# A second buffer for the output weights' pieces, one attention buffer less, and pooled operands issued behind copies

## The chip, the cores and the metric

The kernel runs on one core of a Trainium2 chip. The metric is the device time of one execution in microseconds (us). The engines carry the profile's names: PE is TensorE (matrix products), PEld its weight loads, DVE is VectorE, ACT is ScalarE, POOL is GpSimd, and SP is the engine that issues most of the DMAs. Engines run side by side and wait for each other by semaphores. Within one engine, instructions run in the order in which they were laid out when the program was built, so an instruction that waits holds up all that stand behind it on its engine.

## The reference, cut to what matters

One decoder layer over 1024 tokens of width 2048, all in float32. Every name below is an input or an intermediate of the reference.

```python
h = jnp.einsum('bsd,dc->bsc', x, w_in) + b_in
q, k, v, g_attn, u_pool, g_pool = jnp.split(h, SPLIT_POINTS, axis=-1)
a = banded_sink_attention(q, k, v, sinks, bias_hqk, valid) * jax.nn.silu(g_attn)
b = multiscale_pool(u_pool, w_pool, pool_scale) * jax.nn.silu(g_pool)
mix = jnp.einsum('bsc,cd->bsd', jnp.concatenate([a, b], axis=-1), w_out)
ple = jax.nn.sigmoid(jnp.einsum('bsd,de->bse', x, w_gate_ple)) * jnp.einsum('bsp,pd->bsd', p_i, w_ple)
return layer_norm(DEEPNORM_ALPHA * x + mix + ple, ln_gain, ln_bias)
```

The attention has 16 heads of width 64 and 2 key/value heads. Each block of 128 queries sees its own and the previous block of 128 keys, through a mask with a relative-position bias (`bias_hqk`, laid out for the kernel as `rel`), and each head has a sink that enters the softmax's maximum and sum. The pooling mixer takes trailing means over 2, 4, 8 or 16 tokens, subtracts the token and multiplies by a small matrix per group.

## The kernel before

**Products.** Every large product is done in blocks by a scheme with seven block products in place of eight, and every float32 operand is split into a high and a low part (`wh`, `wl`; an operand unit `t3` gives `t3h`, `t3l`), so that one block product is three matmuls for each of four slices of the inner dimension: 12 matmuls of 128x512 into a PSUM bank `qa` or `qb` (`mm3`, L180 to L185; `product`, L463). A `Job` is a pair of output blocks over half of the inner dimension; `run_group` (L441) runs the seven products of one job, or the fourteen of two jobs in turn. The operand units of the left side are `b11`, `b21`, `t1`, `t2`, `t3`, `b22`, `t4`, used in this order (`BESIDE`, L48, where `t1` and `t2` may change places).

After its last product into a bank, the bank is copied or added into the tile `part` (`gather`, L418 to L425: a copy on ScalarE for the first, an addition on VectorE for the others). The bank can be used again when that has been done.

**Weights.** A job's two weight blocks are loaded into tiles `raw` by SP (`feed_raw`, L194; five buffers), summed and subtracted in place on VectorE (`three_sums`, L206), and split into `wh` (a cast on ScalarE, L816) and `wl` (a subtraction on VectorE, L126) four products ahead of their use (`make_unit`, L215; `take`, L248).

**The clock.** `self.clock` counts products. `after(n, fn)` (L159) runs `fn` when n more products have been written out; `later(n, fn)` (L167) does the same, but ties each instruction of `fn` behind the instruction last recorded on its own engine (`mark`, L134: the last product's matmul on PE, and the last copies on ACT and additions on DVE). The code is thus interleaved by hand into the product loop. Each instruction then gets its place on its engine from a planner that works when the program is built: it goes by the order of the code, but it may put an instruction ahead of others whose operands or buffers are not free yet. `issue_after` is what `later` uses to forbid that.

**Stages.** The products for q, k and v come first. In the attention stage, from about 180 to 700 us, the products go on while other work is hung between them:

- 16 calls of `heads` (L575), one every 9 products, each for four heads and 256 queries. One call: `begin` loads the queries and the two masks (`bias`, from `in_rel`); `split` splits the queries; `score` (L604) multiplies queries by keys into bank `sc`, and VectorE adds the mask and takes the maximum (L616); `shift`, `softmax` and `share` make the shares; `trans` (L644) transposes them into bank `tr`, splits them and masks out their older half on GpSimd (L656); `value` (L659) multiplies by the values into bank `pv`. The steps from `score` on come twice, for n = 0 and n = 1, 4 products apart. All of its buffers are taken from the pool `slots0`, 15 buffers of 128x512 float32 in rotation.
- `centre_weights` (L937) takes the mean over the output columns off `w_out`. It loads `w_out` in 32 pieces of 256 KB into a tile `cw` and sums each on VectorE (`add_up`, L948, line L950), then loads the 32 pieces again, subtracts the mean and stores them as `wc` (`centre`, L956). One piece is fetched every 2 products (every 2 or 3 in the second pass), and used 2 products behind its fetch; the pool `cw` has one buffer.

The third stage makes the gates, the pooling and the embeddings, and ends at about 1107 us. The fourth stage multiplies by the first half of `w_out`; its left operands, the pooled ones, are made by `set_by_twos` (L395) during the last 21 products of the third stage and the first 14 of the fourth. `make_pooled` is the list of its seven steps, for the units in the order above, at the products (10, 13, 16, 19, 22, 28, 31) counted from 21 products ahead of the fourth stage (L1336 to L1338). A step splits a unit (two casts of 128x1024 on ScalarE, two subtractions on VectorE) and issues the loads of the unit two places on. The fifth and sixth stages multiply by the centred half, `wc`, and the norm follows.

`self.ones` (L1268) is a tile of ones that `norm_sums` (L1023) multiplies by, of which it reads one column.

Of the kernel before, what the change touches and what calls it, by code (L numbers as in the profile page):

```python
# [24 lines left out]
F32 = mybir.dt.float32  # L25
# [6 lines left out]
P = 128  # L32
T = 512
H = 4 * P
# [31 lines left out]
class Layer:  # L66
# [203 lines left out]
    def two(self):  # L270
        return self.tile(self.twos, [P, 2, self.F], "two")
# [303 lines left out]
    def heads(self, h, j, half):  # L575
# [9 lines left out]
        def begin():  # L585
            f = slice(h * T + 256 * half, h * T + 256 * half + 256)
            q = self.slot()[:, :T]
            rq.append(q)
            for i in range(2):
                self.load(two(q)[:, i], self.qd[j + i][:, f])  # L590
            for i in range(2):
                bias.append(self.slot()[:, :T].rearrange("p (e k) -> p e k", e=2))
                self.load(bias[i], self.rel[j + i])
# [10 lines left out]
        def score(n, i):  # L604
            s = sc[n, i] = self.slot()[:, :T].rearrange("p (e k) -> p e k", e=2)
            ps = self.bank("sc", 2, (P, 2, 256))
            z = P if none(n) else 0

            keys = slice((4 * h + block(n) - 1) * P + z, (4 * h + block(n) + 1) * P)
            for e in range(2):  # L610
                q = qs[e][:, 256 * i + n * P : 256 * i + n * P + P]
                for k, kk in enumerate(self.kk):
                    nc.tensor.matmul(ps[:, e, z:], q, kk[:, keys], start=k == 0, stop=k == 1)  # L613
            for e in range(2):
                c = 4 * n + 2 * i + e
                nc.vector.tensor_tensor_reduce(  # L616
                    out=s[:, e, z:], in0=ps[:, e, z:], in1=bias[i][:, e, z:], op0=ALU.add, op1=ALU.max, scale=1.0,
                    scalar=self.c(C_SINK + 8 * (j + i) + 2 * block(n) + e), accum_out=mx[:, c : c + 1])
# [19 lines left out]
        def share(n, i):  # L638
            cur = sc[n, i][:, :, P:]
            for e in range(2):  # L640
                c = 4 * n + 2 * i + e
                nc.scalar.activation(cur[:, e], cur[:, e], AF.Copy, scale=rec[:, c : c + 1])
# [16 lines left out]
        def value(n):  # L659
            ps = self.bank("pv", 1)  # L660
            ms = [(self.vv[h][:, block(n)], t) for t in pt[n]]
            if not none(n):
                ms += [(self.vd[h][:, block(n) - 1 + h], t) for t in old[n]]
            for i, (w, t) in enumerate(ms):
                nc.tensor.matmul(ps, w, t, start=i == 0, stop=i == len(ms) - 1)  # L665
            if not pre:
                pre.append(two(self.slot()[:, :T]))
            low = self.slot()[0:64, :T]
            nc.scalar.copy(out=low, in_=ps[64:128])
            hi, low = (t.rearrange("p (i e q) -> p i e q", i=2, e=2) for t in (ps[0:64], low))  # L670
            for e in range(2):
                self.tt(pre[0][64 * e : 64 * e + 64, :, n * P : n * P + P], hi[:, :, e], low[:, :, e], ALU.add)
            if n:
                f = slice(h * T + 256 * half, h * T + 256 * half + 256)
                for i in range(2):
                    self.load(self.pre[j + i][:, f], pre[0][:, i])

        begin()
        self.later(3, split)
        for n in range(2):  # L680
            for i in range(2):
                self.after(6 + 4 * n, lambda n=n, i=i: score(n, i))
            self.after(9 + 4 * n, lambda n=n: shift(n))
            self.after(15 + 4 * n, lambda n=n: trans(n))
            for i in range(2):
                self.after(10 + 4 * n, lambda n=n, i=i: softmax(n, i))
                self.later(12 + 4 * n, lambda n=n, i=i: share(n, i))
            self.after(21 + 4 * n, lambda n=n: value(n))


    def gate_ahead(self, j):
# [245 lines left out]
    def centre_weights(self, at, by):  # L937

        nc = self.nc
        cells = [(b, h) for b in range(NB) for h in range(2)]  # L940
        sums = self.fix.tile([P, 8, NB], F32, name="wsum")
        mean = self.fix.tile([P, 8], F32, name="wmean")
        now = []

        def fetch(b, h):
            now.append(self.load(self.tile(self.cw, [P, H], "cw"), self.wout[b, 0][:, h * H : h * H + H]))

        def add_up(b, h):  # L948
            k = now.pop().rearrange("p (k m) -> p k m", k=4)
            nc.vector.reduce_sum(sums[:, 4 * h : 4 * h + 4, b : b + 1], k, axis=mybir.AxisListType.X)  # L950

        def take_mean():
            nc.vector.reduce_sum(mean.rearrange("p (k b) -> p k b", b=1), sums, axis=mybir.AxisListType.X)
            nc.vector.tensor_scalar(out=mean, in0=mean, scalar1=1.0 / D, scalar2=None, op0=ALU.mult)

        def centre(b, h):  # L956
            w = now.pop()
            k = w.rearrange("p (k m) -> p k m", k=4)
            m = mean[:, 4 * h : 4 * h + 4].rearrange("p (k m) -> p k m", m=1).broadcast_to([P, 4, P])
            self.tt(k, k, m, ALU.subtract)  # L960
            self.load(self.wc[b, 0][:, h * H : h * H + H], w)

        for step in (add_up, centre):
            for c in cells:
                self.after(at, lambda c=c: fetch(*c))
                self.later(at + 2, lambda c=c, step=step: step(*c))
                at += by if step is centre and c[0] % 3 else 2
            if step is add_up:
                self.later(at + 1, take_mean)
                at += 2  # L970

    def split_total(self, total, w, cut):
# [50 lines left out]
    def norm_sums(self, sums, a, first, last):  # L1023

        for b in range(a.shape[-1] // P):
            self.nc.tensor.matmul(sums[:, b : b + 1], a[:, b * P : (b + 1) * P], self.ones[:, 0:1], start=first and b == 0, stop=last,
                                  skip_group_check=True)

    def norm_scale(self, L, wait=0):
# [55 lines left out]
    def run(self):  # L1085
        nc, tc, fix = self.nc, self.tc, self.fix
# [101 lines left out]
        parts, work, over = ExitStack(), ExitStack(), ExitStack()  # L1188
# [76 lines left out]
        self.turn.clear()  # L1265
        self.ident = fix.tile([P, P], F32, name="ident")
        make_identity(nc, self.ident)
        self.ones = fix.tile([P, P], F32, name="ones")  # L1268
        nc.gpsimd.memset(self.ones, 1.0)
        self.mhalf = fix.tile([P, 8], F32, name="mhalf")  # L1270
        nc.gpsimd.memset(self.mhalf, -0.5)
# [10 lines left out]
        work = ExitStack()  # L1282
        self.new_part = lambda b: self.tile(pp, [P, 2, T], "part")
        self.slot_n = T
        self.slots = self.work_pool("slots0", 15, work)
        self.kv = self.work_pool("kv", 1, over)

        def build_kv(b, build, group, halves=(0, 1)):
# [24 lines left out]
        for i in range(n3):  # L1313
            if i == 1:
                over.close()
                work.close()
                work, over = ExitStack(), ExitStack()
                self.slot_n = T + 16
                self.slots = self.work_pool("slots", 16, work)
                self.extras = self.work_pool("e2", 6, over)  # L1320
            if self.groups[g + i + 1][0][0].b[0] == 4 and i < n3 - 2:
                self.after(5, self.embed_in)
                self.after(7, lambda: self.embed_w(2))
            if i == n3 - 2:

                over.close()
                work.close()
                work = ExitStack()
                self.slot_n = T
                six[:] = 5 * [pp] + 3 * [self.work_pool("p8", 3, work)]  # L1330
                self.slots = self.work_pool("slots1", 8, work)
                self.twos = self.work_pool("twos1", 4, work)
                self.new_part = part_of_six
                for n, b in enumerate(s3[-4].b + s3[-3].b):
                    self.after((1, 1, 5, 6)[n], lambda b=b: self.gate_ahead(b - GA0))
                pooled()  # L1336
                for n, step in enumerate(make_pooled):
                    self.after((10, 13, 16, 19, 22, 28, 31)[n], step)  # L1338
                for n, b in enumerate(b for j in s3[-2:] for b in j.b):
                    self.after(16 + 2 * n, lambda b=b: self.gate_ahead(b - GA0))  # L1340
            first = self.groups[g + i][0][0]
            if first.w is wgate and first.b[0] in (4, 6, 8, 10):
                self.pool_sums(*divmod(first.b[0] // 2 - 2, 2), kept_pool)
            self.run_group(g + i, () if i else steps)
# [25 lines left out]
        for i in range(n4):  # L1370
            if i == 1:
                work.close()
                work = ExitStack()
                at = next(i for i, p in enumerate(six) if p is not pp)
# [155 lines left out]
```

## Time and profile before

| What | Value |
|---|---|
| Median of 3 runs | 1445.88 us |
| The three runs | 1445.77, 1445.88, 1448.65 us |
| The profiled execution, its own time | 1448.33 us |
| Its span, first to last instruction | 1446.6 us |
| PE, DVE, ACT, POOL busy | 1429.2, 1115.5, 792.1, 232.8 us |
| DMA moved | 311.86 MB, 216 GB/s over the span |
| Granted TensorE clock, mean | 0.996 |

A row of a group or of the timeline names start and duration in us, the engine, the line of the kernel, the operation, and output `<-` inputs by the program's tile names; a bracket at the end gives the idle time of that engine just before the instruction, and whose signal ended it. A row of the waits names who waited for whom, then the total in us, the count and the longest. A row of the windows names a stretch of the span, then for PE, PEld, DVE, ACT and POOL the busy us and the count of instructions, and then the granted clock, the DMA engines' busy share and GB/s. Durations of matmuls overlap: the distance from one matmul's start to the next is what a matmul costs.

### The profile page before, as it was taken

How to read it: one execution, taken by the hardware profiler on the slowest of the kernel's cores; microseconds unless marked ns; L12 is line 12 of the kernel's file. 1: busy time of each engine (PE TensorE's matmuls, PEld its weight loads, DVE VectorE, ACT ScalarE, POOL GpSimd, SP SyncE). 2: the span in 40 equal slices, each digit the busy share in tenths (PEclk: the TensorE clock that was granted, in tenths of full speed). 3: DMA queues.
4: the chain of work that ended last, by engine and by line, in shares of the span. 5: the costliest groups of instructions: out<-in, count | busy, mean ns of one | idle time of the engine just before them, and what ended most of it. 6: DMA issues, size and time to landing. Idle time of an engine off the chain costs nothing.

```text
span 1446.6 us, 20400 instructions
## 1 busy us (share of the span) xinstructions
PE 1429.2 (99%) x6820; PEld 1210.5 (84%) x6820; DVE 1115.5 (77%) x2045; ACT 792.1 (55%) x1565; POOL 232.8 (16%) x339
## 2 busy tenths in 40 slices
PE   9999999999999999999999999999999999999996
PEld 7888887888888888888888888888888888899996
DVE  6859567787788877878768876867678665987787
ACT  6546375665667656665664444443356433654476
POOL 0000202211122211212111211211001211111223
PEclk9999999999999999999999999999999999999998
DMA  9463877455456655566887869998699768494566
GB/s 358 180 240 120 233 204 225 154 180 177 159 192 200 206 176 184 196 212 211 219 248 210 227 206 287 343 274 266 193 303 308 218 179 232 131 280 111 118 238 228
DMA packets 119226, 311.86 MB, mean 216 GB/s; under 512 B 13585, under 2 KB 27281, under 8 KB 119121
## 3 DMA queue, kind: packets, MB, share of 16 engines
q1 hardware_dynamic: 94480, 230.08, 46.5%
q0 software_dynamic: 21312, 73.15, 21.4%
q10 hardware_dynamic: 3328, 7.34, 1.5%
q8 instruction: 53, 0.87, 0.2%
q14 instruction: 53, 0.43, 0.1%
HBM read 211.95 MB, written 98.57 MB: 215 GB/s over the span
## 4 chain that ended last, share of the span: by engine, by line
PE 90%; DMA 4%; issue 2%; DVE 2%; ACT 1%; POOL 0%; POOLq 0%; SPq 0%; DVEq 0%; ACTq 0%
PE qa L183 15%; PE qa L185 15%; PE qa L184 15%; PE qb L185 11%; PE qb L183 11%; PE qb L184 11%; DMA part<-r 2%; PE sc L613 2%; PE pv L665 2%; DMA cw<-in_wout 2%; PE sc L185 1%; PE sc L183 1%; PE sc L184 1%; PE tr L649 1%; DVE wl L126 0%
## 5 line engine op out<-in xcount | busy, mean ns | idle before, releaser
L816 ACT CAST wh<-raw 128x512 fp32r<-128x512 f32 x428 | 264.3, 619 | 402.9 <-PE qa L184 156.6
L126 DVE TENSOR_TENSOR wl<-raw,wh 128x512 fp32r<-128x512 f32 x428 | 295.2, 693 | 105.2 <-ACT wh L816 100.3
L423 ACT COPY part<-qa 128x512 f32<-128x512 f32 (+1 forms) x180 | 104.0, 578 | 83.9 <-PE qa L185 81.5
L126 DVE TENSOR_TENSOR part<-part,qb 128x512 f32<-128x512 f32 (+1 forms) x120 | 81.1, 676 | 45.2 <-PE qb L185 40.6
L183 PE MATMUL qa<-b11h,wh 128*128 128x512 f32 (+2 forms) x292 | 108.9, 373 | 0.4 <-ACT part L423 0.4
L183 PE MATMUL qb<-b21h,wh 128*128 128x512 f32 (+2 forms) x292 | 108.9, 373 | 0.0
L185 PE MATMUL qa<-b11h,wl 128*128 128x512 f32 (+2 forms) x292 | 108.7, 372 | 0.0
L185 PE MATMUL qb<-b21h,wl 128*128 128x512 f32 (+2 forms) x292 | 108.7, 372 | 0.0
L184 PE MATMUL qa<-b11l,wh 128*128 128x512 f32 (+2 forms) x292 | 108.6, 372 | 0.0
L184 PE MATMUL qb<-b21l,wh 128*128 128x512 f32 (+2 forms) x292 | 108.5, 372 | 0.0
L183 PE MATMUL qa<-t3h,wh 128*128 128x512 f32 (+1 forms) x260 | 100.5, 387 | 2.2 <-ACT part L423 2.2
L184 PE MATMUL qa<-t3l,wh 128*128 128x512 f32 (+1 forms) x260 | 100.3, 386 | 0.0
L185 PE MATMUL qa<-t3h,wl 128*128 128x512 f32 (+1 forms) x260 | 100.3, 386 | 0.0
L183 PE MATMUL qa<-t2h,wh 128*128 128x512 f32 (+1 forms) x260 | 100.1, 385 | 0.1
L183 PE MATMUL qb<-t1h,wh 128*128 128x512 f32 (+1 forms) x260 | 99.9, 384 | 0.0
L185 PE MATMUL qa<-t2h,wl 128*128 128x512 f32 (+1 forms) x260 | 99.8, 384 | 0.0
L183 PE MATMUL qb<-b22h,wh 128*128 128x512 f32 (+1 forms) x260 | 99.7, 384 | 0.0
L185 PE MATMUL qb<-t1h,wl 128*128 128x512 f32 (+1 forms) x260 | 99.7, 384 | 0.0
L185 PE MATMUL qb<-b22h,wl 128*128 128x512 f32 (+1 forms) x260 | 99.7, 383 | 0.0
L185 PE MATMUL qa<-t4h,wl 128*128 128x512 f32 (+1 forms) x260 | 99.7, 383 | 0.0
L183 PE MATMUL qa<-t4h,wh 128*128 128x512 f32 (+1 forms) x260 | 99.6, 383 | 0.0
L184 PE MATMUL qb<-t1l,wh 128*128 128x512 f32 (+1 forms) x260 | 99.6, 383 | 0.0
(336 smaller groups left out, 3494.3 us busy)
## 6 DMA issues: line engine op xcount, KB each, us to landing
raw<-in_win SPq DMA_DIRECT2D x65, 512.0 KB, 4.2
h<-part SPq DMA_DIRECT2D x34, 512.0 KB, 3.0
part<-h POOLq DMA_DIRECT2D x34, 512.0 KB, 6.6
cw<-in_wout SPq DMA_DIRECT2D x64, 256.0 KB, 3.0
raw<-in_wgate SPq DMA_DIRECT2D x32, 512.0 KB, 4.9
raw<-wc SPq DMA_DIRECT2D x32, 512.0 KB, 4.4
s<-in_x SPq DMA_DIRECT2D x44, 256.0 KB, 5.7
s<-in_rel SPq DMA_DIRECT2D x32, 256.0 KB, 4.3
```

Of the source, the lines that this page charges most:

```text
L126: return (eng or self.nc.vector).tensor_tensor(out=out, in0=a, in1=b, op=op)
L183: mm(ps, wh, xh, start=start, stop=False, skip_group_check=True)
L184: mm(ps, wh, xl, start=False, stop=False, skip_group_check=True)
L185: return mm(ps, wl, xh, start=False, stop=stop, skip_group_check=True)
L423: self.mark("ACT", self.nc.scalar.copy(out=dst, in_=ps))
L613: nc.tensor.matmul(ps[:, e, z:], q, kk[:, keys], start=k == 0, stop=k == 1)
L649: nc.tensor.transpose(ps[:, o : o + P], sc[n, i][:, e, P:], self.ident)
L665: nc.tensor.matmul(ps, w, t, start=i == 0, stop=i == len(ms) - 1)
L816: ins = self.nc.scalar.copy(out=out, in_=a)
```

## The change

Five edits.

1. `centre_weights` gets a second buffer, the pool `cw2`; `fetch` takes the two in turn, and `now` becomes a queue, first in, first out. Each piece is used three products behind its fetch in place of two (`add_up` and `centre`), and `take_mean` comes one product later.
2. The pool `slots0` has 14 buffers in place of 15.
3. In `heads`, the two mask loads leave `begin` and come two products later; `value` comes one product earlier, for n = 0 and n = 1.
4. The steps that split the pooled units `b22` and `t4` are hung in with `later` in place of `after`, at products 27 and 30 in place of 28 and 31.
5. `self.ones` is 128x1 in place of 128x128, and `norm_sums` takes it whole.

```diff
@@ heads
             for i in range(2):
                 self.load(two(q)[:, i], self.qd[j + i][:, f])
+
+        def masks():
             for i in range(2):
                 bias.append(self.slot()[:, :T].rearrange("p (e k) -> p e k", e=2))
                 self.load(bias[i], self.rel[j + i])
...
         begin()
+        self.after(2, masks)
         self.later(3, split)
...
-            self.after(21 + 4 * n, lambda n=n: value(n))
+            self.after(20 + 4 * n, lambda n=n: value(n))
@@ centre_weights
-        now = []
+        now, cws = [], [self.cw, self.cw2]
 
         def fetch(b, h):
-            now.append(self.load(self.tile(self.cw, [P, H], "cw"), self.wout[b, 0][:, h * H : h * H + H]))
+            cws.append(cws.pop(0))
+            now.insert(0, self.load(self.tile(cws[0], [P, H], "cw"), self.wout[b, 0][:, h * H : h * H + H]))
...
                 self.after(at, lambda c=c: fetch(*c))
-                self.later(at + 2, lambda c=c, step=step: step(*c))
+                self.later(at + 3, lambda c=c, step=step: step(*c))
                 at += by if step is centre and c[0] % 3 else 2
             if step is add_up:
-                self.later(at + 1, take_mean)
+                self.later(at + 2, take_mean)
                 at += 2
@@ norm_sums
-            self.nc.tensor.matmul(sums[:, b : b + 1], a[:, b * P : (b + 1) * P], self.ones[:, 0:1], start=first and b == 0, stop=last,
+            self.nc.tensor.matmul(sums[:, b : b + 1], a[:, b * P : (b + 1) * P], self.ones, start=first and b == 0, stop=last,
                                   skip_group_check=True)
@@ run
-        self.ones = fix.tile([P, P], F32, name="ones")
+        self.ones = fix.tile([P, 1], F32, name="ones")
...
-        self.slots = self.work_pool("slots0", 15, work)
+        self.slots = self.work_pool("slots0", 14, work)
+        self.cw2 = self.work_pool("cw2", 1, work)
...
                 for n, step in enumerate(make_pooled):
-                    self.after((10, 13, 16, 19, 22, 28, 31)[n], step)
+                    (self.later if n > 4 else self.after)((10, 13, 16, 19, 22, 27, 30)[n], step)
```

## The prediction

> **What bounds the kernel now.** I read the page's first part, then TensorE's waits, then three windows around the largest of them.
>
> ```profile
> span 1446.6 us, 20400 instructions
> PE 1429.2 (99%) x6820; PEld 1210.5 (84%) x6820; DVE 1115.5 (77%) x2045; ACT 792.1 (55%) x1565; POOL 232.8 (16%) x339
> PE qa L183 <- ACT part L423: 2.7, 2, 2.2
> ...
> PE sc L613 <- DVE st L616: 0.3, 1, 0.3
> 230.00:235.00 5.00, 4.40 (x20) 3.31 (x18) 4.93 (x16) 1.57 (x7) 0.29 (x1) 1.00 0.94 232
> 235.00:240.00 5.00, 3.35 (x8) 2.68 (x9) 2.04 (x7) 4.68 (x10) 1.15 (x2) 0.68 0.95 235
> 240.00:245.00 5.00, 5.00 (x28) 4.24 (x28) 4.10 (x12) 1.20 (x2) 1.61 (x2) 0.98 0.86 326
> ```
>
> TensorE is busy for 99% of the span, so only its pauses can be won. The waits left out of the list are those of the kernel's first and last steps, which the diff leaves alone, and some of at most 0.2 us. The L183 waits are two (total, count and longest in us): one near 236 us, where the granted clock (the column after POOL's) also falls to 0.68, and a small one. This is the first:
>
> ```profile
> 229.50 0.69 DVE L950 TENSOR_REDUCE wsum<-cw 128x4 f32<-128x512 f32 x1 [2.20 <-DMA cw<-in_wout]
> 233.43 0.21 ACT L625 ACTIVATE st<-st 128x4 f32<-128x4 f32 x1 [3.76 <-DVE st L126]
> 234.01 0.39 PE L185 MATMUL qb<-t1h,wl 128*128 128x512 f32 x1
> 236.02 0.57 ACT L423 COPY part<-qa 128x512 f32<-128x512 f32 x1
> 236.65 0.67 PE L183 MATMUL qa<-t3h,wh 128*128 128x512 f32 x1 [2.25 <-ACT part L423]
> 237.11 0.63 PE L184 MATMUL qa<-t3l,wh 128*128 128x512 f32 x1
> 240.40 0.39 PE L183 MATMUL qa<-t3h,wh 128*128 128x512 f32 x1
> 1107.26 0.39 PE L184 MATMUL qa<-t4l,wh 128*128 128x512 f32 x1
> 1107.48 0.39 PE L185 MATMUL qa<-t4h,wl 128*128 128x512 f32 x1
> ```
>
> Read backwards. TensorE needs bank qa, which ScalarE copies out at 236.02. ScalarE had stood 3.76 us for VectorE's softmax shift. VectorE had stood 2.20 us before the reduction of a weight piece whose load had not landed. An undisturbed step from matmul to matmul is 0.22 to 0.23 us (last two rows); I use 0.227, so a product of 12 matmuls is 2.72 us. The pause costs 236.65 - 234.01 - 0.23 = **2.41 us**. The nine steps to 240.40 take 3.75 us in place of 9 x 0.227 = 2.04: **1.71 us** at the lower clock.
>
> The Trainium skill, page "TensorE: Matmul & The Clock Gate", section "Part 1: The HAM clock gate", puts the halving behind an idle window of about 3.4 us. By that section, 2.25 us of idleness would not lower the clock, and the 1.71 us would have another cause and stay. Here the first long step stands right behind the pause, so the row goes against the page's figure.
>
> **The change part by part.** *Second buffer cw2, use three products behind the load.* These rows are the landing times of the tile cw, waits of VectorE (190 to 240 us) and SP (190 to 720 us), and the chain of waits:
>
> ```profile
> DMA to landing us min/median/max: 2.0/2.9/9.3
> DVE wsum L950 <- DMA cw<-in_wout: 7.2, 4, 3.6
> SPq L140 <- DMA cw<-in_wout: 71.4, 31, 9.0
> SPq L140 <- PE pv L665: 21.2, 8, 6.3
> 202.57 9.30 DMA cw<-in_wout
> 270.50 0.95 PE sc L613 x8
> 286.51 0.95 PE sc L613 x8
> 299.80 0.96 PE sc L613 x8
> ```
>
> Scores of one kind come every 9 products: 299.80 - 270.50 = 29.3 us, or 3.26 us per product with attention in it. With one buffer, a load may start only behind the reduction placed at the same tick, and its own reduction stands two products later: at most 6.5 us, less whatever VectorE is late. The four loads of the crowded stretch took up to 9.3 us, so VectorE stood 7.2 us. With two buffers the load waits for a reduction placed one product earlier, and is used 3 x 3.26 = 9.8 us behind its place. Even 9.3 us fits. The last wait alone, 2.20 us, is nearly the pause; with all 7.2 us gone the copy at 236.02 comes before TensorE asks. I count -2.41 and -1.71. What is late next is VectorE's own list, 4.93 of 5 us busy from 230 to 235: a few tenths could stay. SP, which stood 71.4 us on cw, issues what is queued behind it sooner. Number and size of the 64 loads, 32 reductions and 32 stores do not change. Each use moves by one product, past what SP issues in that product; the centred pieces are then stored a product later, and the stage that reads them begins hundreds of us behind. No cost.
>
> *14 attention buffers, masks later, value one product earlier.* A head takes 9 products before the next begins. Two mask buffers held two products less and eight share buffers held one less are 12 buffer-products per 9 products, or 1.3 buffers of demand, against the one taken away. The mask's lead:
>
> ```profile
> 264.86 1.79 SPq L140 DMA_DIRECT2D s<-in_rel  x2
> DMA to landing us min/median/max: 2.8/4.3/9.3
> 299.36 0.44 PE tr L649 x4
> 319.47 0.92 PE pv L665 x4
> ```
>
> The masks issued at 264.86 serve the scores at 286.51, 21.6 us later. Two products (6.5 us) off leaves 15.1, against at most 9.3 to landing (the second row is that of the masks). On SP the two loads of each of the 16 heads move past what two products issue there (a cw piece, weight blocks, stores of `h`); nothing is added. `value` takes its two `pre` stores along, a product earlier. The values of the transposes at 299.36 run at 319.47, 20 us behind; one product less is 17. Between stand a cast, a subtraction and two selections on GpSimd, which is busy 16% of the span. Cost nothing; if that cover failed, TensorE would pause at L665. The order on each engine is laid out when the program is built, and this shifts it: the trace of before can't show the new one. Bounds: from -0.4 us (the 0.3 us score wait goes, with its step) to +4.1 us for one new pause of the kind at 236. I take 0, the nearer row, since in all the rest of the attention stage TensorE waits once, for 0.3 us.
>
> *Pooled operands b22 and t4 behind copies.* The small wait:
>
> ```profile
> 1106.70 1.05 ACT L816 CAST b22h<-two 128x1024 fp32r<-128x1024 f32 x1 [2.62 <-DMA two<-cc]
> 1107.65 0.58 ACT L423 COPY part<-qa 128x512 f32<-128x512 f32 x1
> 1108.28 0.50 PE L183 MATMUL qa<-b11h,wh 128*128 128x512 f32 x1 [0.41 <-ACT part L423]
> 1108.62 0.39 PE L184 MATMUL qa<-b11l,wh 128*128 128x512 f32 x1
> 1107.78 1.23 DVE L126 TENSOR_TENSOR b22l<-two,b22h 128x1024 fp32r<-128x1024 f32 x1 [2.44 <-ACT b22h L816]
> 1135.63 0.39 PE L183 MATMUL qb<-b22h,wh 128*128 128x512 f32 x1
> ```
>
> The second of b22's two casts waits 2.62 us for its operand, and the bank copy queues behind it. The loss is 1108.28 - 1107.48 - 0.23 = 0.57 us, and 0.11 in the step behind it. `later` ties the casts behind the copies recorded by then, and so adds a wait: behind it on ScalarE queue casts of weight units, which are made four units ahead. The operands' loads are issued by earlier steps and do not move. The 27th product falls six into the stage begun at 1108.28, at 1124.6; two casts and the last subtraction (2 x 1.05 + 1.23 = 3.3 us) fit before 1135.63. t4 at the 30th (1132.8) is needed two products after b22, at 1141.1. So **-0.6 us**, a tenth left for a bank's handing over. If that cover failed, TensorE would pause there for some tenths instead: 0 net.
>
> *ones, one column wide.*
>
> ```profile
> L1269 POOL MEMSET ones<- x1: 205/205/205, 0.9 to 0.9; 128x128 f32 x1
> ```
>
> By the code the matmuls read one column already. 0.2 us of fill on GpSimd lie beside the first weight loads. Nothing.
>
> **Sum.** -2.41 - 1.71 - 0.6 = -4.7 us on the profiled execution's 1448.33 (1446.6 of span and 1.7 around it): **1443.6 us**. The runs shown lie at 1445.77, 1445.88 and 1448.65. The profiled one belongs with the highest; the 2.45 us to the median are the size of the slow clock (1.71) and a part of the pause. I read that as a pause that lowers the clock in some executions only. Against the median 1445.88 the forecast is -0.16%. A measurement of this kernel tells about 0.2%, or 2.9 us, from no change: faster begins below 1443.0, slower above 1448.8.
>
> **The rivals.**
>
> *The pause is not what the runs differ by.* Then the median holds all 4.7 us, and the time is 1445.88 - 4.7 = 1441.2. For it: no trace of a short run is shown. Against: the sizes match.
>
> *SP is held by a mask instead* (the slower side). With 14 buffers a mask's load waits on SP for a buffer that `value` frees, and weight blocks queue behind it:
>
> ```profile
> 283.45 0.33 SPq L140 DMA_DIRECT2D raw<-in_win  x1
> 289.24 1.11 DVE L126 TENSOR_TENSOR s<-raw 128x512 f32<-128x512 f32 x1
> raw<-in_win SPq DMA_DIRECT2D x65, 512.0 KB, 4.2
> ```
>
> A block issued at 283.45 is summed at 289.24, 5.8 us later, and lands in 4.2. Held by more than 1.6 us, it stops VectorE as the cw piece did. Price: 2.41 + 1.71 = 4.1 us each. One gives 1447.7; from two on it is slower: 1443.6 + 8.2 = 1451.8. For it: SP already stands up to 6.3 us for `pv`. Against: demand falls by 1.3 buffers for the one taken, and the cw holds on SP go.
>
> *The change does not cure the wait.* From 230 to 240 us the DMA engines are 0.94 to 0.95 busy; a load issued sooner may land no sooner, and the reductions still stop VectorE. Then only 0.6 us come off: 1447.7 on the profiled execution. Against: 9.8 us of lead over 9.3.
>
> *The lower clock has another cause.* Then only the pauses go: 1448.33 - 2.41 - 0.6 = 1445.3. That is also what the page's 3.4 us would give (the Trainium skill, as above). Against: the step that grows from 0.23 to 0.46 us right behind the pause.
>
> **How the numbers follow.** Forecast 0.58, its own range 1442.5 to 1444.8 (the 0.4 us score wait and a few tenths left at 236, some tenths between runs). Runs not split by the pause 0.15. SP held once 0.06, twice or more 0.10. Not cured 0.07. Other cause of the clock 0.04. Faster: 0.15 and the forecast's lower edge, 0.17: 0.32. Slower: 0.10. Same: 0.58. The range 1441.2 to 1447.7 leaves out the twice-held case and half of the first rival, some 0.18.
>
> **What would show it.** Right: no wait of VectorE for cw from 190 to 240 us, SP's 71.4 us for cw down to a few, a granted clock of 1.00 from 235 to 240, no L183 wait for L423 at 236 or 1108, and b22h cast after 1120. Wrong: a wait of TensorE at L613, L649 or L665 in the attention stage, weight blocks waited for by VectorE, SP waits for `pv` above 21 us, or a pause at the use of b22 or t4.

## The result, and the profile after

The kernel after takes 1443.13 us (median of 9 runs, 1441.48 to 1444.74), the kernel before, run beside it, 1446.87 (9 runs, 1445.77 to 1450.37). The ratio is 0.9967, with a 95% interval of 0.9955 to 0.998: some 0.2 to 0.45% faster. The forecast of 1443.6 is 0.5 us off, and the range holds the time. But the gain, 0.33%, is twice the forecast's 0.16%, and beyond the 0.2% that it had called no change.

The profiled execution of after took 1443.51 us. The page's first part:

```profile
span 1441.8 us, 20390 instructions
PE 1426.6 (99%) x6820; PEld 1209.0 (84%) x6820; DVE 1114.6 (77%) x2045; ACT 792.8 (55%) x1565; POOL 237.7 (16%) x339
```

TensorE's waits from 100 to 1440 us (total, count, longest):

```profile
PE sc L1058 <- POOL st L126: 1.1, 1, 1.1
PE tr L551 <- ACT s L557: 0.9, 1, 0.9
PE qa L183 <- ACT part L423: 0.3, 1, 0.3
PE qb L183 <- DVE part L126: 0.3, 1, 0.3
PE qb L183 <- ACT t2h L819: 0.3, 1, 0.3
PE pv L1030 <- ACT t2l L1021: 0.2, 1, 0.2
PE qa L183 <- ACT wh L819: 0.2, 1, 0.2
```

The lines of the kernel have moved by two to four: L819 was L816, L954 was L950. The row of 2.7 us, L183 behind the copy of L423, has become 0.3 us, at 484. The first row stands in the kernel's end in both kernels. The second ends at 194, ahead of the place that the change was made for; two traces with none of the edits at that place have it too (e3 and e11 below, 1.0 and 0.9 us), so it is not the change's. The wait in L613 for the maximum (L615 <- L618 here) is gone. All the other waits are of 0.2 to 0.3 us.

The three windows around the old pause (columns as before):

```profile
230.00:235.00 5.00, 5.00 (x24) 4.14 (x23) 2.95 (x9) 4.92 (x12) 1.66 (x2) 1.00 0.87 250
235.00:240.00 5.00, 5.00 (x30) 4.30 (x29) 3.14 (x6) 2.33 (x5) 0.76 (x2) 1.00 0.89 308
240.00:245.00 5.00, 5.00 (x24) 4.07 (x23) 4.91 (x16) 0.65 (x2) 0.58 (x1) 1.00 0.39 131
```

The last link of the old chain, in ScalarE's timeline the copy, and in TensorE's the step into the bank:

```profile
232.47 0.58 ACT L423 COPY part<-qa 128x512 f32<-128x512 f32 x1
```

```profile
234.41 0.39 PE L185 MATMUL qb<-t1h,wl 128*128 128x512 f32 x1
234.63 0.39 PE L183 MATMUL qa<-t3h,wh 128*128 128x512 f32 x1
```

TensorE is busy for 5.00 of 5 us in each, at a clock of 1.00. The copy starts at 232.47, which was 236.02, and the step from one bank to the other is 0.22 us. VectorE, 4.93 busy from 230 to 235 before, is at 2.95. That is no work saved (1114.6 us in all, 1115.5 before): the work that stood behind the late piece was done earlier.

The landing times of the tile `cw`:

```profile
DMA to landing us min/median/max: 2.0/3.0/8.1
```

SP's waits from 190 to 720 us:

```profile
SPq L140 <- DVE wsum L954: 55.3, 19, 7.8
SPq L140 <- PE pv L667: 15.9, 6, 4.3
SPq L140 <- DMA cw<-in_wout: 3.8, 2, 2.4
```

The pieces land hardly sooner (8.1 us at most, 9.3 before). VectorE waits for none of them from 190 to 240: the trace has no such row there. SP's 71.4 us for them are down to 3.8, but SP now stands 55.3 us for the reductions that free the two buffers, where this row of the trace before says 28.0:

```profile
SPq L140 <- DVE wsum L950: 28.0, 19, 6.0
```

Other rows have grown too (the waits for `part` from 52.6 to 78.9 us), and all of SP's waits together are 387.8 us, 399.5 before. So SP stands hardly less: the holds have moved to other rows. What the second buffer bought is that the hold lies on the load's side, ahead of the use, and not on VectorE's.

The start of the fourth stage, now at 1104.3, in ScalarE's and TensorE's timelines:

```profile
1115.26 1.15 ACT L699 ACTIVATE part<-part,cst 128x1024 f32<-128x1024 f32 x1 [3.31 <-DMA part<-h]
1122.19 2.00 ACT L819 CAST b22h<-two 128x1024 fp32r<-128x1024 f32 x2
```

```profile
1118.39 0.47 PE L183 MATMUL qb<-t1h,wh 128*128 128x512 f32 x1 [0.29 <-DVE part L126]
```

The casts of `b22h` have gone to 1122, behind two copies, and no wait is left at the stage's start. A small one stands 14 us later: a gate's operand lands late, ScalarE waits 3.31 us, and an addition on VectorE and a bank come 0.29 us late.

### Where the time went

I set the starts of the first matmul of the same products in two traces side by side. Before was traced four times in all, after twice (the further ones are experiments below). Lengths in us, in the order profiled execution, e5, e10, e11, and profiled execution, e8; the places are those of the first trace of before:

| Stretch | Before | After | Difference of means |
|---|---|---|---|
| start to 195.6 | 195.57, 194.71, 195.66, 196.10 | 195.88, 195.56 | +0.2 |
| 195.6 to 248.4 | 52.83, 48.77, 50.15, 50.17 | 48.85, 48.86 | -1.6 |
| 248.4 to 691.4 | 443.01, 444.42, 444.14, 444.45 | 442.89, 442.46 | -1.3 |
| 691.4 to 1102.3 | 410.86, 410.82, 410.90, 411.10 | 411.28, 410.99 | +0.2 |
| 1102.3 to 1130.2 | 27.92, 27.98, 29.19, 28.91 | 27.75, 27.58 | -0.8 |
| 1130.2 to 1431.2 | 301.01, 300.25, 301.76, 301.76 | 299.91, 299.67 | -1.4 |

The sum is -4.7 us; the medians differ by 3.7, and by 3.5 in a second comparison (e8). Three of the four traced executions of before (1448.33, 1444.13, 1448.96, 1449.65 us) are among its longer ones, so the differences are rather too large. The old pause is a third of the sum, not 4.1 us of it.

### The profile page after: what moved, and what is told of

It reads as the page before. It is cut to its first block, busy times and chain, and to the rows that moved or that the text cites. A ratio compares the mean times of both kernels' runs of the same rounds, so it can differ in the third digit from the quotient of the medians.

```text
span 1441.8 us, 20390 instructions
## 1 busy us (share of the span) xinstructions
PE 1426.6 (99%) x6820; PEld 1209.0 (84%) x6820; DVE 1114.6 (77%) x2045; ACT 792.8 (55%) x1565; POOL 237.7 (16%) x339
## 4 chain that ended last, share of the span: by engine, by line
PE 95%; DMA 2%; DVE 1%; ACT 1%; issue 1%; POOL 0%; SPq 0%; POOLq 0%; DVEq 0%; ACTq 0%
PE qa L183 16%; PE qa L185 16%; PE qa L184 16%; PE qb L183 12%; PE qb L185 12%; PE qb L184 12%; PE sc L615 2%; PE pv L667 2%; PE sc L185 1%; PE sc L184 1%; PE sc L183 1%; PE tr L651 1%; DMA part<-h 1%; DMA s<-t 0%; DMA raw<-in_win 0%
## 5 line engine op out<-in xcount | busy, mean ns | idle before, releaser
L819 ACT CAST wh<-raw 128x512 fp32r<-128x512 f32 x428 | 264.6, 620 | 407.3 <-PE qa L184 152.1
L423 ACT COPY part<-qa 128x512 f32<-128x512 f32 (+1 forms) x180 | 103.8, 577 | 82.7 <-PE qa L185 80.5
L183 PE MATMUL qb<-b21h,wh 128*128 128x512 f32 (+2 forms) x292 | 108.8, 373 | 0.0
L183 PE MATMUL qa<-b11h,wh 128*128 128x512 f32 (+2 forms) x292 | 108.7, 372 | 0.0
L183 PE MATMUL qb<-t1h,wh 128*128 128x512 f32 (+1 forms) x260 | 100.1, 385 | 0.5 <-DVE part L126 0.3
L183 PE MATMUL qa<-t2h,wh 128*128 128x512 f32 (+1 forms) x260 | 100.1, 385 | 0.2 <-ACT wh L819 0.2
L183 PE MATMUL qa<-t3h,wh 128*128 128x512 f32 (+1 forms) x260 | 99.9, 384 | 0.3 <-ACT part L423 0.3
L183 PE MATMUL qb<-b22h,wh 128*128 128x512 f32 (+1 forms) x260 | 99.8, 384 | 0.0
L183 PE MATMUL qa<-t4h,wh 128*128 128x512 f32 (+1 forms) x260 | 99.7, 383 | 0.0
```

Of the source, the lines that this page charges most:

```text
L183: mm(ps, wh, xh, start=start, stop=False, skip_group_check=True)
L423: self.mark("ACT", self.nc.scalar.copy(out=dst, in_=ps))
L819: ins = self.nc.scalar.copy(out=out, in_=a)
```

## The experiments

Two theories at first. **A**: the late weight piece makes the pause, and the second buffer cures it. **B**: the pause goes because edits 2 to 4 place VectorE's work elsewhere, and the buffer is not needed.

### e1_cw_only: edits 1, 2 and 5, without 3 and 4

```diff
@@ before
-        now = []
+        now, cws = [], [self.cw, self.cw2]
...
-            now.append(self.load(self.tile(self.cw, [P, H], "cw"), self.wout[b, 0][:, h * H : h * H + H]))
+            cws.append(cws.pop(0))
+            now.insert(0, self.load(self.tile(cws[0], [P, H], "cw"), self.wout[b, 0][:, h * H : h * H + H]))
...
-                self.later(at + 2, lambda c=c, step=step: step(*c))
+                self.later(at + 3, lambda c=c, step=step: step(*c))
...
-        self.slots = self.work_pool("slots0", 15, work)
+        self.slots = self.work_pool("slots0", 14, work)
+        self.cw2 = self.work_pool("cw2", 1, work)
...
```

The lines left out at the end are those of `take_mean` and of edit 5.

> The kernel before with the second cw buffer, use three products behind, 14 attention buffers and the narrow ones; masks, value and the pooled steps stay as before. Theory (the cw piece makes the pause near 236 us, and the mask and value edits are only there to give the buffer back): VectorE's waits for cw from 190 to 240 us fall from 7.2 to under 2 us, the pause of 2.25 us and the clock of 0.68 are gone, the small pause at 1108 us (0.4 us) stays; 3 to 4 us under the before of the same call. Rival (14 buffers do not carry the old mask and value places): TensorE pauses at L613, L649 or L665, or the SP queue is held by masks, and at least half of the gain goes back.

1444.28 us (11 runs) against 1445.98 (29 runs of before, which the first four experiments share): ratio 0.9986, 0.9977 to 0.9995. VectorE waits for no piece from 190 to 240, TensorE does not pause at 236, and none of the attention stage's lines appears among its waits, although the masks and `value` stand at their old places and have a buffer less. So by the trace 14 buffers carry both. The gain is 1.7 us, not the 3 to 4 that I expected; the time alone would also fit the rival, but e7 below, with the same places and buffers and edit 4 besides, gains 3.0.

The trace also tells why the wait is gone. These are the landing times of the pieces from 190 to 240 us in e1:

```profile
DMA to landing us min/median/max: 2.5/5.5/9.0
```

The slowest of them takes 9.0 us (9.2 in e7), nearly as long as the 9.3 of before, and VectorE waits for none. The pieces do not land sooner; their loads are issued early enough.

### e2_one_piece: everything but the second buffer

```diff
@@ after
-        now, cws = [], [self.cw, self.cw2]
+        now = []
...
-            cws.append(cws.pop(0))
-            now.insert(0, self.load(self.tile(cws[0], [P, H], "cw"), self.wout[b, 0][:, h * H : h * H + H]))
+            now.append(self.load(self.tile(self.cw, [P, H], "cw"), self.wout[b, 0][:, h * H : h * H + H]))
...
-                self.later(at + 3, lambda c=c, step=step: step(*c))
+                self.later(at + 2, lambda c=c, step=step: step(*c))
...
-                self.later(at + 2, take_mean)
+                self.later(at + 1, take_mean)
...
-        self.cw2 = self.work_pool("cw2", 1, work)
```

> The kernel after with the second cw buffer undone: one buffer, use two products behind; 14 attention buffers, later masks, earlier value and pooled steps behind copies stay. Theory: the pause comes back, VectorE waits 5 us or more for cw from 190 to 240 us, the granted clock dips there, and the time is that of before less 0.6 us for the small pause at 1108 us: 0.1% under before or not to be told from it. Rival (the mask loads at the head of the SP queue made the pause, and moving them cures it): no pause, 3 us under before.

1446.23 us (1444.06 to 1450.70, 11 runs) against 1445.98: ratio 1.0001, 0.9991 to 1.0011. Without the second buffer the whole gain is gone. But the profiled execution, 1445.3 us, does not show the old pause. Of VectorE's waits from 190 to 240 us, the one for the pieces:

```profile
DVE wsum L953 <- DMA cw<-in_wout: 1.9, 2, 1.7
```

TensorE's waits from 100 to 1440 us:

```profile
PE qa L183 <- ACT part L423: 1.9, 1, 1.9
...
PE qb L183 <- DVE part L126: 0.6, 1, 0.6
```

VectorE waits for pieces, but for 1.9 us in place of 7.2, and TensorE feels nothing of it at 236. TensorE's row of 1.9 us stands at 485, in the second pass over the weights. VectorE's timeline ahead of it:

```profile
468.14 0.70 DVE L126 TENSOR_TENSOR cw<-cw,wmean 128x512 f32<-128x512 f32 x1 [2.42 <-DMA cw<-in_wout]
...
482.00 1.24 DVE L126 TENSOR_TENSOR cw<-cw,wmean 128x512 f32<-128x512 f32 x1
```

A piece was late at 468, and a later subtraction stands at 482.00. In after, the pause there is 0.30 us. That the second pass's pieces make the pause at 485 is likely by these rows, but no run took it by itself. The trace of e9, with the same edits and wider loads, has it again (1.81 us at 486).

Theory A has the time for it, and B falls in this: the buffer is needed. That the loss has to be at 236 is not borne out. Whether edits 2 to 4 make the wait at 236 smaller too stays open: neither trace with them and one buffer (e2, e9) has a pause there, but one execution of before (e5) has none either.

### e4_two_close: both buffers, each piece used two products behind its load

```diff
@@ after
-                self.later(at + 3, lambda c=c, step=step: step(*c))
+                self.later(at + 2, lambda c=c, step=step: step(*c))
...
-                self.later(at + 2, take_mean)
+                self.later(at + 1, take_mean)
```

> The kernel after, but each piece used two products behind its fetch in place of three; both buffers stay. Theory A (what counts is that the load no longer waits for the reduction of the same product): pieces that land within 6.5 us are in time, only the slowest (up to 9.3 us) make VectorE wait, under 3 us in all from 190 to 240 us, and TensorE's pause is under 0.5 us; within 0.1% of after. Theory B (the distance of three products counts as much): VectorE still waits 4 us or more there and a pause over 1 us stays, with the clock's dip.

1442.56 us (7 runs), ratio 0.9973, 0.9963 to 0.9984: not told from after. VectorE waits for no piece from 190 to 240. So it is the buffer that counts, which lets a load start earlier; the third product in the change's name adds nothing that can be measured.

### e3_pooled_only: edit 4 alone

```diff
@@ before
-                    self.after((10, 13, 16, 19, 22, 28, 31)[n], step)
+                    (self.later if n > 4 else self.after)((10, 13, 16, 19, 22, 27, 30)[n], step)
```

> The kernel before with the pooled steps of b22 and t4 behind copies, at 27 and 30, and nothing else. Theory: the L183 wait for the copy of L423 at the start of the fourth stage (0.41 us, 0.68 with its steps) is gone, all else as before, pause near 236 us included: 0.6 us under before, which the time can hardly show but the trace can. Rival (the casts only move the wait): a wait of like size stands at a product within 40 us behind the stage's start.

1445.73 us (11 runs), ratio 0.9995, 0.9986 to 1.0003: a gain of 0.25 us, between 2.0 and a loss of 0.4, so too small for these times to show. The trace does show it: TensorE has no wait between 1095 and 1125, and the stretch from 1102 to 1130 takes 27.24 us. Over all traces the six without edit 4 have a mean of 28.46 there (27.92 to 29.19), the eight with it 27.69 (27.20 to 28.38): -0.8 us, where I had put a price of 0.6. The pause at 236 stays, as it must, at 0.7 us and with no fall of the clock:

```profile
235.20 0.50 PE L183 MATMUL qa<-t3h,wh 128*128 128x512 f32 x1 [0.68 <-ACT part L423]
```

### e5_before_again, e10_before_third, e11_before_fourth: the kernel before, traced again

The forecast rests on one reading that no trace had shown: runs of before differ because the pause lowers the clock in some of them. Three more traces, with no edit.

> The kernel before, unchanged, for a second trace of it. Theory (the pause near 236 us differs from execution to execution, and lowers the clock in some only): TensorE's wait for the copy of L423 near 236 us is between 0 and 3 us, and its size plus the time lost at the lower clock goes with the execution's time: under 1446 us no dip of the clock, above 1448 us a dip. Rival (the pause is always the same and the executions differ elsewhere): 2.25 us and a clock near 0.68 again, whatever the time.

> The kernel before, a third trace. From the traces so far (cw waits of 7.2, 4.5, 3.2 us in programs that are alike up to there, with pauses of 2.25, 0.68 and 0 us): the pause grows from 0 at waits of some 3.5 us; a clock dip only with a pause of 2 us or more, and then an execution above 1447 us.

> The kernel before, a fourth trace, for the same: pause by cw waits, clock dip by pause, and time by dip.

They took 1444.13, 1448.96 and 1449.65 us. The windows from 235 to 240, first of e5, then of e10, then of e11:

```profile
235.00:240.00 5.00, 5.00 (x29) 4.31 (x28) 4.34 (x12) 1.65 (x3) 1.61 (x2) 1.00 0.93 326
```

```profile
235.00:240.00 5.00, 4.39 (x25) 3.84 (x26) 2.14 (x4) 4.70 (x8) 0.54 (x2) 1.00 0.87 292
```

```profile
235.00:240.00 5.00, 3.97 (x22) 3.38 (x23) 2.06 (x6) 5.00 (x8) 0.72 (x1) 1.00 0.93 246
```

The clock column says 1.00 in all three, in the two longest executions too. The reading falls: the lower clock was seen once in four traces of before, and not in the longest. What the traces do show is a pause whose size follows VectorE's wait. The waits of VectorE from 190 to 240 in e5, e10 and e11:

```profile
DVE wsum L950 <- DMA cw<-in_wout: 3.2, 4, 1.9
```

```profile
DVE wsum L950 <- DMA cw<-in_wout: 5.1, 3, 2.3
```

```profile
DVE wsum L950 <- DMA cw<-in_wout: 5.0, 3, 2.5
```

With 3.2 us of waiting TensorE stands 0 us near 236, with 5.1 and 5.0 it stands 1.1, with 7.2 (the first trace) 2.25; e3, with 4.5, has 0.68; e2 and e9, with 1.9 and 2.6, have 0. By these numbers the slack of the chain is a good 3 us, and TensorE feels somewhat more than half of what goes beyond 3.2 us: 0.68 of 1.3, 1.1 of 1.9, 2.25 of 4.0. The chain of the prediction is right, and its dose differs from execution to execution.

The two long executions lose the rest in several small places. TensorE's waits in e10 from 100 to 1440 us:

```profile
PE qa L183 <- ACT part L423: 2.7, 3, 1.4
PE sc L1054 <- POOL st L126: 1.1, 1, 1.1
PE sc L613 <- DVE st L616: 0.9, 1, 0.9
```

The first row has the same 2.7 us as the page of before, but in three pauses, which end at 236, 486 and 1108, and the longest is that at 1108. Two executions with one row alike can have lost their time in different places: the count and the longest are to be read with the sum.

### e6_late_centre: the same load, but 16 products later

To take the pieces out of the crowded stretch and leave the single buffer, the centring is begun at product 24 and not 8.

```diff
@@ before
-        self.centre_weights(8, 3)
+        self.centre_weights(24, 3)
```

> The kernel before, with one cw buffer, but the weight pieces begin 16 products later (at 24 in place of 8), behind the place of the pause. Theory (the loads of cw, short of buffers in a crowded stretch, stop VectorE and so make the pause): no wait for cw and no pause of more than 0.3 us from 190 to 240 us; the time falls by 1 to 3 us against before. Rival (the stage's own start, with key and value building and the first heads, is too much for VectorE and ScalarE): a pause of 0.6 us or more stays near 236 us without any cw work there.

1450.28 us (12 runs) against 1445.47 (25 runs of before): ratio 1.003, 1.0016 to 1.0043. I expected a gain of 1 to 3 us and it lost 4.8. The pause at 236 is gone, as expected. But the second pass now runs on past the end of the attention stage. Two windows of its trace:

```profile
690.00:695.00 5.00, 4.26 (x12) 3.42 (x13) 5.00 (x9) 3.77 (x8) 0.00 (x0) 0.66 0.98 343
725.00:730.00 5.00, 2.47 (x11) 1.76 (x10) 2.30 (x4) 3.42 (x4) 0.00 (x0) 1.00 0.79 176
```

TensorE's two largest waits from 100 to 1440 us:

```profile
PE qb L183 <- DVE part L126: 3.2, 1, 3.2
PE qa L185 <- DVE wl L126: 2.5, 1, 2.5
```

VectorE's wait for the pieces from 670 to 740:

```profile
DVE cw L126 <- DMA cw<-in_wout: 16.1, 4, 8.4
```

VectorE waits 16.1 us for four pieces, while the DMA engines are 0.98 busy (first window). TensorE's two pauses end at 691, behind an addition out of a bank, and at 729, behind a part of a weight unit. The second stands right behind the longest of the waits, 8.4 us, which ends at 727.7. For the first the link is longer: the waits of 3.7 us each end at 670 and 678, and VectorE is then nearly always busy until that addition, at 690. This is the mechanism of 236 us at another place, with another last link, shown directly for the second pause and argued for the first: a reduction or subtraction whose piece is late stops whatever VectorE has behind it. My error was to take the load for hidden where it was moved to.

### e9_wide_piece: a larger dose at the old place

e2 with 384 KB in place of 256 KB for each of the first 16 pieces, of which the kernel uses 256 KB.

```diff
@@ e2_one_piece
-            now.append(self.load(self.tile(self.cw, [P, H], "cw"), self.wout[b, 0][:, h * H : h * H + H]))
+            w = self.tile(self.cw, [P, H + 256], "cw")
+            fetch.n += 1
+            if fetch.n <= 16:
+                self.load(w, self.wout[b, 0][:, h * 256 : h * 256 + H + 256])
+                now.append(w[:, h * 256 : h * 256 + H])
+            else:
+                now.append(self.load(w[:, :H], self.wout[b, 0][:, h * H : h * H + H]))
+
+        fetch.n = 0
```

> The kernel of e2 (one cw buffer, the other edits in), where the first 16 pieces are loaded with 384 KB in place of 256 KB; what is added to the load is not used. It raises the suspected cost alone. Theory (VectorE's waits for cw, and nothing else, make the pause near 236 us): the waits for cw from 190 to 240 us, 1.9 us in the trace of e2, rise to 5 us or more, a pause of 1 us or more stands near 236 us, and the time is 1 us or more above before. Rival (the waits for cw only go along with a crowded stretch): the waits rise, and TensorE has no pause over 0.3 us near 236 us.

1446.32 us (11 runs) against 1445.42 (21 runs of before): ratio 1.0008, 0.9998 to 1.0018. VectorE waits 2.6 us for pieces from 190 to 240, little more than e2's 1.9, and TensorE does not pause at 236. I expected 5 us or more. The dose was too small, below the slack of 3 us: the run tells theory and rival apart as little as it tells the price of the pause.

### e7_old_places and e8_after_again: edit 3 undone, and after itself beside it

```diff
@@ after
-        def masks():
...
-        self.after(2, masks)
...
-            self.after(20 + 4 * n, lambda n=n: value(n))
+            self.after(21 + 4 * n, lambda n=n: value(n))
```

> The kernel after, with masks and value at their old places (14 buffers, two cw buffers and the pooled steps stay). Theory (the mask and value edits are not needed and cost a pause near 483 us, 0.57 us in the trace of after): that pause is gone, none of over 0.3 us comes in the attention stage, and the time is 0 to 0.7 us under after. Rival (with 14 buffers the old places cost waits): 1 us or more above after.

> The kernel after, unchanged, beside the others on the same chip: 3 to 4 us under before; no pause near 236 us; the pauses near 192 us (a wait for an accumulating DMA ahead of it on ScalarE) and 483 us differ from the first trace by up to 1 us each.

Edit 3 undone: 1442.45 us (1441.96 to 1442.96, 10 runs), ratio 0.9972, 0.9962 to 0.9983 with 1445.47 beside it; after: 1441.98 (1441.29 to 1443.45, 10 runs), ratio 0.997, 0.996 to 0.998. They are not told apart: the later masks and the earlier `value` are worth nothing that can be measured. From 190 to 1130 us the trace of e7 has a single wait of TensorE:

```profile
PE qb L183 <- DVE part L126: 0.2, 1, 0.2
```

The pause at 484 is gone, as expected. With two buffers it stands, at 0.3 to 0.4 us, in the traces that have edit 3 (after twice, and e4) and in none that lacks it (e1, e7, e12). And e1 and e7 differ by edit 4 alone: 1.7 and 3.0 us, each against its own runs of before. So edit 4 may be worth some 1.3 us beside the second buffer, where alone (e3) it gains 0.25; the two intervals overlap, so this is a hint and not shown.

### e12_wait_more: e7 with more lead at the start of the fourth stage

A try at the small wait that is left at 1117 (1118 in after): the last blocks of the third stage wait one product more.

```diff
@@ e7_old_places
-            j.wait = 5 if j in s3[-4:-1] else 6 if j is s3[-1] else 4
+            j.wait = 5 if j in s3[-4:-2] else 6 if j is s3[-2] else 7 if j is s3[-1] else 4
```

> The kernel of e7 (masks and value at their old places) in which the last four blocks of the third stage wait one product more for their accumulating loads. Theory (the pause left near 1117 us is a gate on ScalarE that waits for such a load, with a bank's addition late behind it): that pause, 0.3 us in e7, goes, and nothing else changes: 0.3 us under e7, 3 to 4 us under before, not to be told from after by its time. Rival (the bank is late for another reason, or the later gates delay what follows them): the pause stays or another of like size comes.

1442.71 us (11 runs), ratio 0.998, 0.997 to 0.9989 against 1445.42. The wait is gone, and the stretch from 1102 to 1130 is the shortest of all traces (27.20 us), but the time is not told from that of after or of e7. No version here beats after by what can be measured.

## Why the prediction was right or wrong

**What bounds the kernel**: right in the main. TensorE is 99% busy in both, and most of the gain came from its pauses. But that "only its pauses can be won" is too narrow: some 0.8 us came from shorter steps between matmuls (see `ones` below).

**The second buffer**: right in the mechanism, mis-sized in the sum. e1 and e4 show that with the second buffer VectorE's waits for the pieces and the pause are gone, and e2 that without it the gain is gone. The rival that the change does not cure the wait falls with them. But the two terms, -2.41 and -1.71, are those of the one execution in which the pause was largest and the clock fell. In the four traces of before the stretch is 4.0, 0, 1.3 and 1.3 us over that of after: 1.6 in the mean, for 4.1.

**"I read that as a pause that lowers the clock in some executions only"**: this is the step that failed. e10 and e11 are longer than the profiled execution, with a clock of 1.00. The runs differ by several pauses of 0.2 to 1.4 us and by up to 1.5 us in the last stages. The rival that the runs are not split by this pause was right on that point; but its price, all 4.7 us off the median, was wrong too, since the median never held 4.1 us of pause. The rival that the lower clock has another cause falls only in part: it is 1.00 in after, where the pause is gone, and in e6 it fell behind a pause at another place; but e10 and e11 have the pause without it.

**Masks, `value` and 14 buffers at nothing**: right by the times for the places (e7), and by the traces of e1 and e7 for the buffers. The rival of a load held by a mask falls: SP's waits for `pv` went down from 21.2 to 15.9 us, VectorE waits for no weight block, and no wait of TensorE is in the attention stage stands at L615, L651 or L667 (L613, L649 and L665 before). The edge of the bound, -0.4 us for the wait of the score, was nearer than the middle: the stretch from 642 to 691, where it stood, is 0.5 us shorter in the mean. But edit 3 is not what took this wait away: it is gone in e1 and e7 too, at the old places.

**The pooled operands, -0.6**: right; -0.8 in the traces. The copies that now go first are there, and the late use is in time: no wait at `b22` or `t4`. What came late next was the gate at 1115, which cost 0.29 us at 1118.

**`ones` (and the smaller pool) at nothing in the last stages**: too low. From 1322 to 1431 us, eight traces of kernels with edits 2 and 5 take 108.06 to 108.10 us, the six without them 108.42 to 109.27. No pause holds this time. From 1322 to 1385 us (places again those of the first trace of before), at a granted clock of 1.00, the mean step between matmuls of 128x384 is 0.1734 to 0.1735 us in those eight traces and 0.1744 to 0.1767 in the six: the prediction had put a term at nothing that sits in the steps. Why they are shorter is open, and no run had one of the two edits without the other.

So 1443.6 is near the time by luck: its errors offset each other. By the forecast the median held 1445.88 - 1443.6 = 2.3 us of what the change takes away. The traces show 1.6 for the pause, 0.8 for the pooled operands, 0.5 at the score and 0.8 from 1322 on, 3.7 of the table's 4.7, each a mean over few executions; the medians say 3.5 and 3.7. That the four terms come out at the same sum is partly chance, since the traced executions of before are longer than its median. The start helped as well: the median of before in the comparison was 1446.87, 1.0 us above the 1445.88 that the forecast had, and in the second comparison after took 1441.98, below the forecast's own range. The edits do not add up either: e1 gains 1.7 us, edit 4 alone 0.25, edits 2 to 5 together (e2) nothing, all of them 3.5 to 3.7. With one buffer, what the other edits gain was taken back elsewhere, in the traces of e2 and e9 by the pause at 485.

## What to carry to other kernels

A small background task on a busy in-order engine is paid for by whatever stands behind it: give its load a second buffer before moving the work, and look at the stretch into which a move carries it. A term read from one execution is the size of that execution; before it is set against a median, ask for more traces, and read the count and the longest wait beside the sum. Slack hides a late load up to a point (here some 3 us of VectorE's time), so a dose below it proves nothing.

## What the runs showed of the hardware

The lower clock does not follow from the length of the pause alone. It fell to 0.68 behind a pause of 2.25 us in the first trace of before, and to 0.66 in e6 behind 3.22, where the first step is 0.56 us in place of 0.227. These are TensorE's rows there:

```profile
690.74 0.77 PE L183 MATMUL qb<-t1h,wh 128*128 128x512 f32 x1 [3.22 <-DVE part L126]
691.30 0.63 PE L184 MATMUL qb<-t1l,wh 128*128 128x512 f32 x1
```

Behind the 2.5 us of e6 (window 725 to 730, above) and the 1.9 us of e2 it stayed at 1.00. The Trainium skill, page "TensorE: Matmul & The Clock Gate", section "Part 1: The HAM clock gate", says that activity is watched in a free-running window of about 3.4 us, so that the point at which the clock changes depends on where in the window the first matmul lands. A fall behind 2.25 us and none behind 2.5 would agree with that, if the place of a pause in the window matters in the same way; no run here shows the window. They do not agree with the same section's reading that the lower clock comes after at least one idle window: the pauses ahead of these falls were shorter.

The executions of kernels with the second buffer also spread less: each group of 7 to 11 runs lies within 1.0 to 3.3 us, and each group of the kernels with one buffer, of 9 to 29 runs, within 3.5 to 7.8. e7's ten runs lie within 1.0 us, the 25 of before beside them within 6.3 (1444.44 to 1450.76).
